# The first products of a conditioned trunk layer: conditioning one k-tile ahead, seven early load places in one ring, whole-float32 products for the first four k-tiles

## The chip, the cores and the metric

The kernel runs on one core of one Trainium2 chip. The metric is the device time of one execution in microseconds (us). TensorE (PE) does the matmuls, VectorE (DVE) and ScalarE (ACT) the elementwise work, GpSimd (POOL) a few small operations, and SyncE (SP) issues the loads from HBM. Each engine takes its instructions in the order in which they were recorded for it and waits where an operand isn't there yet.

## The reference, cut to what matters

One layer on x of 256 tokens by 2048 channels, float32, with one conditioning vector c:

```python
c_act = silu(c)
shift1, scale1, gate1, shift2, scale2, gate2 = split(c_act @ w_ada + b_ada, 6)   # w_ada 2048 x 12288
h = rms_norm(x, norm1_g) * (1 + scale1) + shift1
proj = h @ w_in + b_in                                # w_in 2048 x 8192
a_in, s_in, gates = split(proj, [2048, 4096])         # a: GLU, s: u and v, gates: 4096 wide
...                                                   # conv, LayerNorm, spatial mixing, merge
x = x + gate1 * (merged @ w_out)
...                                                   # up projection, conv, silu, down projection
```

The change lies in the first two lines (of which shift1 and scale1 are needed for h) and in the first part of h @ w_in.

## The kernel before, in words

All matrices are tiled by 128. The 2048 channels are 16 k-tiles; h is kept transposed, one tile of 128 channels by 256 tokens for each k.

A float32 product is made of three matmuls in a reduced type, float32r: an operand is split into a high part, rounded, and a low part, the rest (`split`, L135 to L137: ACT writes hi at L136, DVE lo at L137). `mm3` (L157 to L161) multiplies hi by hi, hi by lo and lo by hi into one PSUM tile. `load_raw` (L139 to L142) loads a block of weights, mostly 1 MB, into one of four places of 128 x 2048 with the tag `raw`; a pool gives each load the place that comes free first.

Ahead of the products, cact = silu(c) is spread over 128 partitions by PE and copied to `cbc` by DVE (L111). The mean squares of x are summed by ACT (L213, L214) and DVE (L215), POOL raises them to the power -1/2 (L117), and DVE scales two identity tiles with them, `diag` (L219). PE transposes and scales x by a matmul with diag (L206, tiles `trx`), and ACT copies the result to `xT` (L207), in four parts q = 0 to 3: two ahead of the loop, two inside its first round.

The loop over k ("first products", L304 to L333) then does, for each of the 16 k-tiles:

- two `ada_block`s (L181 load of 1 MB, L182 DVE product with cbc and sum), one for a column of 128 values of scale1 and one for shift1. Their loads go into three places of their own, the slots T5 to T7, in turn.
- gs (L309) and sh (L310) on DVE, h (L312) and its high part hH (L136) on ACT, its low part hL (L137) on DVE.
- the load of the block of weights a (2048 columns for k < 4, 1280 later), and its split into hi_a and lo_a.
- PE's products of that block and h into pa0 to pa3 and pv0, which collect all k; for k < 4 also into pd0 to pd2, which are copied to `gab` after k = 3 (L331).
- the job of that k from `jobs` (L294): for k = 4 to 8 a quarter of the gate's products (`gate_quarter`: load gq, split, 48 matmuls into two tiles pgq; the result goes to gab by an ACT copy at L271 or a DVE sum at L273), for later k such quarters and halves (`half_job`, tiles pg, copy L285).

Behind this loop come v, a, u, g (the other gate halves), so (the spatial branch's output, whole-float32 products straight from its loaded block, L589), co (the convolution branch's output), wo, and then up and down. In them, `pump` interleaves background work: convolution taps, and the other four adaLN blocks, whose loads use the four `raw` places too. A scheduler places the instructions of all this on the engines; their order on each engine is fixed when the program is built.

Of the kernel before, what the change touches and what calls it, by code (L numbers as in the profile page):

```python
# [10 lines left out]
F32 = mybir.dt.float32  # L11
F32R = mybir.dt.float32r
AF = mybir.ActivationFunctionType
ALU = mybir.AluOpType
# [3 lines left out]
P = 128  # L18
D = 2048
S = 256  # L20
NT = S // P
KT = D // P
# [14 lines left out]
NV = 2  # L37
# [3 lines left out]
RAW_BUFS = 4  # L41
# [6 lines left out]
C_BIN = C_BADA + 6 * KT  # L48
# [16 lines left out]
def trunk(ctx, tc, xin, cvec, rows, wada, wa0q, wa0, wa1, wv, wu, wg, wgq0, wgq1, wgq2, wso, wco, wsT, wout, wup0, wup, wdn, out):  # L65
    nc = tc.nc
    ctx.enter_context(nc.allow_low_precision(reason="exact two-part split of float32 operands"))
    keep = ctx.enter_context(tc.tile_pool(name="keep", bufs=1))
    wp = ctx.enter_context(tc.tile_pool(name="wp", bufs=1))
# [3 lines left out]
    def psum(name="ps"):  # L73
        return pp.tile([P, 512], F32, tag="ps", name=name)

    def slot(i, shape, name, dt=F32):

        return keep.tile(shape, dt, tag=f"T{i}", name=name)

    def t1(name, n=S):  # L80
        return tp.tile([P, n], F32, tag="t1", name=name, bufs=7)
# [4 lines left out]
    def small(n, name):  # L86
        return tp.tile([P, n], F32, tag=f"sm{n}", name=name, bufs=4)
# [4 lines left out]
    cv = keep.tile([P, NCOL], F32, tag="cv", name="cv")  # L92
    xs = [slot(t, [P, D], f"xs{t}") for t in range(NT)]
    for t in range(NT):
        nc.sync.dma_start(out=xs[t], in_=xin[:, t, :])
    nc.sync.dma_start(out=cv[:, KT:], in_=cvec[:, KT:])
    ident = keep.tile([P, P], F32, tag="ident", name="ident")
    make_identity(nc, ident)
    ones = keep.tile([P, P], F32, tag="ones", name="ones")
# [6 lines left out]
    def bcast_cols(dst, cols, n, name, copy=nc.scalar.copy):  # L106

        ps = psum(f"bc{name}")
        for i in range(n):
            nc.tensor.transpose(ps[:, i * P:(i + 1) * P], cols[:, i:i + 1].broadcast_to([P, P]), ident)  # L110
        copy(dst, ps[:, :n * P])  # L111

    def rsqrt(dst, v, name):

# [8 lines left out]
    def rms_rstd(ss, name):  # L123

        n = ss.shape[1]
        v = small(n, f"v{name}")
        nc.vector.tensor_reduce(v, ss, axis=AX.X, op=ALU.add)
        nc.vector.tensor_scalar(v, v, 1.0 / D, EPS, op0=ALU.mult, op1=ALU.add)
        r = small(n, f"r{name}")
        rsqrt(r, v, name)  # L130
        return r

    last = {}

    def split(hi, lo, src):  # L135
        nc.scalar.activation(hi, src, AF.Copy)  # L136
        return nc.vector.tensor_tensor(lo, src, hi.bitcast(F32), op=ALU.subtract)  # L137

    def load_raw(src, name):  # L139
        n = src.shape[-1]  # L140
        raw = wp.tile([P, 2048], F32, tag="raw", name=f"raw_{name}", bufs=RAW_BUFS)[:, :n]
        nc.sync.dma_start(out=raw, in_=src)  # L142
        return raw

# [12 lines left out]
    def mm3(ps, wH, wL, aH, aL, start, stop, **kw):  # L157

        nc.tensor.matmul(ps, wH, aH, start=start, stop=False, **kw)  # L159
        nc.tensor.matmul(ps, wH, aL, start=False, stop=False, **kw)  # L160
        nc.tensor.matmul(ps, wL, aH, start=False, stop=stop, **kw)  # L161
# [8 lines left out]
    cact = keep.tile([P, KT], F32, tag="cact", name="cact")  # L170
    nc.scalar.activation(cact, cc, AF.Sigmoid)
    nc.vector.tensor_tensor(cact, cact, cc, op=ALU.mult)
    cbc = keep.tile([P, D], F32, tag="cbc", name="cbc")
    for q in range(4):
        bcast_cols(cbc[:, q * 512:(q + 1) * 512], cact[:, 4 * q:4 * q + 4], 4, f"c{q}", nc.vector.tensor_copy)

    def ada_block(which, j, dst, w=None):

        if w is None:
            w = wp.tile([P, 2048], F32, tag="raw", name=f"ada{which}_{j}", bufs=RAW_BUFS)  # L180
        nc.sync.dma_start(out=w, in_=wada[which, j])  # L181
        nc.vector.scalar_tensor_tensor(w, w, 1.0, cbc, op0=ALU.mult, op1=ALU.mult, accum_out=dst)  # L182

    def ada_cols(which):
        return keep.tile([P, KT], F32, tag=f"mod{which}", name=f"mod{which}")

    def bada(which, a=0, b=KT):
        return cv[:, C_BADA + which * KT + a:C_BADA + which * KT + b]
# [20 lines left out]
    xT = [slot(2 + i, [P, 8, S], f"xT{i}") for i in range(2)]  # L209
    ss1 = tp.tile([P, NT, 2], F32, tag="ss1", name="ss1", bufs=1)  # L210
    nc.gpsimd.memset(ss1, 0.0)
    jk = [keep.tile([P, D], F32, tag=tag, name=f"jk{tag}") for tag in ("hH", "hL")]
    nc.scalar.activation(jk[0], xs[0], AF.Square, accum_out=ss1[:, 0, 0:1])  # L213
    nc.scalar.activation(jk[0][:, :D // 2], xs[1][:, :D // 2], AF.Square, accum_out=ss1[:, 1, 0:1])  # L214
    nc.vector.scalar_tensor_tensor(jk[1][:, D // 2:], xs[1][:, D // 2:], 1.0, xs[1][:, D // 2:], op0=ALU.mult, op1=ALU.mult, accum_out=ss1[:, 1, 1:2])  # L215
    r1 = rms_rstd(ss1, "1")
    diag = keep.tile([P, NT, P], F32, tag="rrow", name="diag")
    for t in range(NT):
        nc.vector.tensor_scalar_mul(diag[:, t, :], ident, r1[:, t:t + 1])  # L219
    for q in range(2):  # L220
        transposes(xs, xT, q, "x", diag)

# [7 lines left out]
    hH = keep.tile([P, KT, S], F32R, tag="hH", name="hH")  # L230
    hL = keep.tile([P, KT, S], F32R, tag="hL", name="hL")
# [4 lines left out]
    pa = [psum(f"pa{j}") for j in range(4)] + [psum(f"pv0{j}") for j in range(NV // 2)]  # L236
    sc1, sh1 = ada_cols(1), ada_cols(0)
# [4 lines left out]
    def gab_of(j):  # L242

        if j // 4 not in gab4:
            gab4[j // 4] = slot((0, 1, 4, 2)[j // 4], [P, 4, 2 * S], f"gab{j // 4}")
        return gab4[j // 4][:, j % 4, :]
# [36 lines left out]
    def half_job(j):  # L283
        def f():
            nc.scalar.copy(gab_of(j), gate_half(j, 0))  # L285
        return f
# [4 lines left out]
    def q1(i):  # L291
        return lambda: gate_quarter((2 * i, 2 * i + 1), 1, wgq1[i]) if i < 5 else gate_quarter((10,), 1, wgq2)

    jobs = {4: [q0(0)], 5: [q0(1)], 6: [q0(2)], 7: [q0(3)], 8: [q1(0), q1(5)], 9: [half_job(11)], 10: [q1(1), half_job(12)],  # L294
            11: [q1(2)], 12: [half_job(13)], 13: [q1(3), half_job(14)], 14: [q1(4)], 15: [half_job(15)]}
    pd = []

    def direct(ps, hi, lo, j, k, last_k):
        for half in range(2):
            cs = slice((2 * j + half) * P, (2 * j + half + 1) * P)  # L300
            mm3(ps[:, half * S:(half + 1) * S], hi[:, cs], lo[:, cs], hH[:, k, :], hL[:, k, :],
                k == 0 and half == 0, k == last_k, skip_group_check=True)

    for k in range(KT):  # L304
        c = slice(k, k + 1)
        for i, (which, dst) in enumerate(((1, sc1), (0, sh1))):
            ada_block(which, k, dst[:, c], slot(5 + (2 * k + i) % 3, [P, 2048], f"ada{which}_{k}"))
        gs, sh = small(1, f"gs{k}"), small(1, f"sh{k}")
        nc.vector.scalar_tensor_tensor(gs, sc1[:, c], bsc1[:, c], cv[:, C_G1 + k:C_G1 + k + 1], op0=ALU.add, op1=ALU.mult)  # L309
        nc.vector.tensor_tensor(sh, sh1[:, c], bada(0, k, k + 1), op=ALU.add)  # L310
        h = t1(f"h{k}")
        nc.scalar.activation(h, xT[k // 8][:, k % 8, :], AF.Identity, scale=gs, bias=sh)  # L312
        split(hH[:, k, :], hL[:, k, :], h)
        src = wa0q[k] if k < 4 else wa0[k - 4]
        n0 = src.shape[-1]
        raw = load_raw(src, f"a{k}")
        hi = wp.tile([P, 2048], F32R, tag="hi", name=f"hi_a{k}", bufs=HI_BUFS)[:, :n0]
        lo = wp.tile([P, 2048], F32R, tag="lo", name=f"lo_a{k}", bufs=HI_BUFS)[:, :n0]
        split(hi, lo, raw)
        for j in range(4 + NV // 2):  # L320
            direct(pa[j], hi, lo, j, k, KT - 1)
        if k == 0:
            for q in range(2, 4):
                transposes(xs, xT, q, "x", diag)
            pd += [psum(f"pd{j}") for j in range(QD)]
        if k < 4:
            for j in range(QD):
                direct(pd[j], hi, lo, 4 + NV // 2 + j, k, 3)
        if k == 3:
            for j in range(QD):  # L330
                nc.scalar.copy(gab_of(j), pd[j])  # L331
        for job in jobs.get(k, ()):
            job()  # L333
    gab = [gab_of(j) for j in range(KT)]


# [64 lines left out]
    def ln_steps():  # L401
# [24 lines left out]
        def s6():  # L426
            bcast_cols(crow, st["rr"], NT, "cr")
# [23 lines left out]
    for which, dst in ((2, g1c), (4, sc2), (3, sh2)):  # L451
        for j in range(KT):
            bg["ada"].append((2.25, lambda which=which, dst=dst, j=j: ada_block(which, j, dst[:, j:j + 1])))
# [32 lines left out]
    for j in range(8):  # L486
        if j < NV:
            ps = pa[4 + j // 2][:, (j % 2) * S:(j % 2 + 1) * S]
        else:
            ps = psum(f"pvc{j}")[:, :S]  # L490
# [54 lines left out]
    for j in range(4, 8):  # L545
        ps = psum(f"pa{j}")
# [18 lines left out]
    for j in range(8):  # L565
        ps = psum(f"pu{j}")
# [7 lines left out]
    for j in range(KT):  # L574
        ps = gate_half(j, 1)
        nc.vector.tensor_tensor(gab[j], gab[j], ps, op=ALU.add)
        pump("g", 5.15, 2.9)
        for half, jj in ((0, J_GA + j), (1, J_GB + j)):
            nc.scalar.activation(gab[j][:, half * S:(half + 1) * S], gab[j][:, half * S:(half + 1) * S], AF.Sigmoid,
                                 bias=cv[:, C_BIN + jj:C_BIN + jj + 1])  # L580


    for j2 in range(8):
        raw = load_raw(wso[j2], f"so{j2}")
        ps = psum(f"pso{j2}")
# [4 lines left out]
        for half in range(2):  # L590
            j = 2 * j2 + half
# [125 lines left out]
    for j in range(KT):  # L717
        bg["ada"].append((2.25, lambda j=j: ada_block(5, j, g2c[:, j:j + 1])))
# [172 lines left out]
```

## Time and profile before

| | |
|---|---|
| median of 3 runs | 1382.54 us (1378.96 to 1382.74) |
| the profiled execution, its own time | 1383.14 us |
| its span | 1381.4 us |
| PE busy | 1337.5 us, 97% |
| DVE, ACT busy | 1073.6 us, 653.4 us |
| mean TensorE clock granted | 0.986 of full speed |

The profile is one execution. In a timeline a row gives the start, the duration, the engine, the line, the operation, its output and inputs, the shape, how many instructions the row stands for, and in brackets how long the engine had been idle before it and what it waited for. In the table of waits the numbers are the microseconds in total, how often, and the longest. A matmul's duration includes its way through the array, so that the distance between two starts, and not the duration, says what one costs in a dense stream.

### The profile page before, as it was taken

What the parts mean: (1) busy time and instruction counts of PE and PEld (TensorE: products, weight loads), DVE (VectorE), ACT (ScalarE), POOL (GpSimd) and SP (SyncE); (2) the same over time, 40 slices, a digit from 0 to 9 for tenths busy, and PEclk for the clock granted to TensorE, in tenths of its full rate; (3) what the DMA queues carried; (4) which work ended last, traced back from release to release, by engine and by line L of the source; (5) the groups of instructions that cost most, each with busy time, mean ns of one, the idle gap of its engine ahead of it and who ended that gap; (6) DMA issues with size and microseconds to landing.
All of it is one profiled execution on the core that took longest, in us unless ns stands there. A gap on an engine that the chain in (4) does not pass through costs nothing.

```text
span 1381.4 us, 19730 instructions
## 1 busy us (share of the span) xinstructions
PE 1337.5 (97%) x8200; PEld 1197.3 (87%) x8200; DVE 1073.6 (78%) x1321; ACT 653.4 (47%) x770; POOL 6.4 (0%) x18
## 2 busy tenths in 40 slices
PE   5799999999999999998999999999999999999997
PEld 5799999999999898887888888888888888888885
DVE  5878899999999798888898887754456776776573
ACT  4344465545541344435555555543334555555451
POOL 0000000000000000000000000000000000000000
PEclk8899999999999999999999999999999999999999
DMA  8988876778786898885887775555555555555551
GB/s 347 361 350 340 362 294 254 263 269 287 294 306 259 307 353 334 318 337 207 298 300 275 276 272 183 185 181 190 199 190 183 186 192 196 188 183 187 192 200 61
DMA packets 49481, 350.89 MB, mean 254 GB/s; under 512 B 5616, under 2 KB 5616, under 8 KB 8176
## 3 DMA queue, kind: packets, MB, share of 16 engines
q1 hardware_dynamic: 49392, 349.63, 68.5%
q8 instruction: 64, 1.05, 0.3%
q14 instruction: 25, 0.20, 0.0%
HBM read 347.51 MB, written 2.10 MB: 253 GB/s over the span
## 4 chain that ended last, share of the span: by engine, by line
PE 90%; DVE 6%; ACT 2%; issue 1%; DMA 1%; POOL 0%; SPq 0%; ACTq 0%; POOLq 0%; DVEq 0%
PE pup L732 24%; PE pup L733 12%; PE pod L166 6%; PE pod L167 6%; PE pod L165 6%; PE pso L589 4%; PE pg L159 2%; PE pg L161 2%; PE pg L160 2%; DVE ada L182 2%; PE powo L167 2%; PE powo L166 2%; PE powo L165 2%; PE pa L160 2%; PE pa L161 2%; PE pa L159 2%
## 5 line engine op out<-in xcount | busy, mean ns | idle before, releaser
L137 DVE TENSOR_TENSOR lo_up<-raw_up,hi_up 128x2048 fp32r<-128x2048 f32 x88 | 201.5, 2290 | 84.6 <-ACT hi_up L136 84.6
L732 PE MATMUL pup<-h2hH,hi_up 128*128 128x512 f32 x704 | 252.6, 397 | 0.9 <-DVE h2hH L228 0.9
L732 PE MATMUL pup<-h2hL,hi_up 128*128 128x512 f32 x704 | 251.0, 395 | 0.0
L182 DVE SCALAR_TENSOR_TENSOR ada<-ada,cbc 128x2048 f32<-128x2048 f32 x96 | 218.3, 2285 | 7.3 <-DMA ada<-in 7.3
L136 ACT ACTIVATE hi_up<-raw_up 128x2048 fp32r<-128x2048 f32 x88 | 168.7, 1917 | 109.9 <-PE pup L732 84.1
L733 PE MATMUL pup<-h2hH,lo_up 128*128 128x256 f32 x704 | 198.6, 282 | 0.0
L733 PE MATMUL pup<-h2hL,lo_up 128*128 128x256 f32 x704 | 197.9, 281 | 0.0
L137 DVE TENSOR_TENSOR lo_d<-raw_d,hi_d 128x2048 fp32r<-128x2048 f32 x42 | 96.3, 2292 | 94.5 <-ACT hi_d L136 94.5
L732 PEld LDWEIGHTS pup<-h2hH,hi_up 128*128 128x128 f32 x704 | 133.2, 189 | 32.9 <-DVE h2hH L228 1.3
L732 PEld LDWEIGHTS pup<-h2hL,hi_up 128*128 128x128 f32 x704 | 132.3, 188 | 31.4
L733 PEld LDWEIGHTS pup<-h2hH,lo_up 128*128 128x128 f32 x704 | 132.9, 189 | 0.0
L136 ACT ACTIVATE hi_d<-raw_d 128x2048 fp32r<-128x2048 f32 x42 | 80.5, 1917 | 109.9 <-PE pod L167 90.4
L733 PEld LDWEIGHTS pup<-h2hL,lo_up 128*128 128x128 f32 x704 | 132.0, 188 | 0.0
L166 PE MATMUL pod<-lo_d,f 128*128 128x512 f32 x332 | 130.2, 392 | 0.0
L167 PE MATMUL pod<-hi_d,f 128*128 128x512 f32 x332 | 130.2, 392 | 0.0
L165 PE MATMUL pod<-hi_d,f 128*128 128x512 f32 x332 | 130.1, 392 | 0.0
L161 PE MATMUL pg<-hH,lo_g 128*128 128x256 f32 x336 | 93.8, 279 | 0.2 <-DVE lo_g L137 0.2
L159 PE MATMUL pg<-hH,hi_g 128*128 128x256 f32 x336 | 94.0, 280 | 0.0
L160 PE MATMUL pg<-hL,hi_g 128*128 128x256 f32 x336 | 93.7, 279 | 0.0
L376 DVE SCALAR_TENSOR_TENSOR yc<-apad,cv,yc 128x256 f32<-128x256 f32 x200 | 84.0, 479 | 0.8 <-ACT yc L374 0.6
L741 ACT ACTIVATE yv<-pl,cv 128x256 f32<-128x256 f32 x88 | 51.0, 597 | 64.1 <-DVE pl L740 64.1
L159 PE MATMUL pa<-hH,hi_a 128*128 128x256 f32 x256 | 69.3, 293 | 8.1 <-ACT hH L136 7.3
(224 smaller groups left out, 2808.1 us busy)
## 6 DMA issues: line engine op xcount, KB each, us to landing
ada<-in SPq DMA_DIRECT2D x96, 1024.0 KB, 5.1
raw_up<-in SPq DMA_DIRECT2D x88, 1024.0 KB, 4.8
raw_d<-in SPq DMA_DIRECT2D x44, 1024.0 KB, 4.8
raw_g<-in SPq DMA_DIRECT2D x21, 1024.0 KB, 5.1
raw_wo<-in SPq DMA_DIRECT2D x16, 1024.0 KB, 5.4
raw_a<-in SPq DMA_DIRECT2D x12, 1024.0 KB, 5.7
raw_gq<-in SPq DMA_DIRECT2D x9, 1024.0 KB, 8.2
raw_u<-in SPq DMA_DIRECT2D x8, 1024.0 KB, 4.8
```

The source lines that it names most:

```text
L136: nc.scalar.activation(hi, src, AF.Copy)
L137: return nc.vector.tensor_tensor(lo, src, hi.bitcast(F32), op=ALU.subtract)
L159: nc.tensor.matmul(ps, wH, aH, start=start, stop=False, **kw)
L160: nc.tensor.matmul(ps, wH, aL, start=False, stop=False, **kw)
L161: nc.tensor.matmul(ps, wL, aH, start=False, stop=stop, **kw)
L165: nc.tensor.matmul(ps, aH, wH, start=start, stop=False, **kw)
L166: nc.tensor.matmul(ps, aH, wL, start=False, stop=False, **kw)
L167: nc.tensor.matmul(ps, aL, wH, start=False, stop=stop, **kw)
L182: nc.vector.scalar_tensor_tensor(w, w, 1.0, cbc, op0=ALU.mult, op1=ALU.mult, accum_out=dst)
L376: nc.vector.scalar_tensor_tensor(ycf[:, j, :], src, cv[:, w0 + k:w0 + k + 1], ycf[:, j, :], op0=ALU.mult, op1=ALU.add)
L732: nc.tensor.matmul(ps, hi, hk.rearrange("p a s -> p (a s)"), start=(k == 0), stop=(k == KT - 1), skip_group_check=True)
L733: nc.tensor.matmul(ps[:, :S], lo, hk[:, 0, :], start=False, stop=(k == KT - 1), skip_group_check=True)
```

## The change

The conditioning of a k-tile (ada blocks, gs, sh, h, hH) becomes a function `condition`, and condition(k + 1) is recorded ahead of the products of k. The weights of k + 1 are loaded and split (`first_weights`) behind the job of k, and hL follows directly behind lo_a (`low_h`); for k < 4, hL stands behind the ada blocks of the next tile.

For k < 4 the weights are not split: one whole-float32 matmul with the loaded block and h takes the place of the three.

All loads of this stage go in turn into seven places, the four `raw` ones and T5 to T7. After the stage the four are used in turn, in the order in which the program asks for them, where a pool chose before.

The first load of cv, the table of small vectors, is cut to the columns that this stage needs; the rest is loaded at k = 3. The square sum of DVE is placed behind the copies to cbc, and the first ada blocks behind diag.

```diff
-    nc.sync.dma_start(out=cv[:, KT:], in_=cvec[:, KT:])
+    nc.sync.dma_start(out=cv[:, KT:C_BIN], in_=cvec[:, KT:C_BIN])
...
+    ring = {"n": 0, "all": RAW_BUFS + 3}
+    def raw_place(name):
+        i = ring["n"] % ring["all"]
+        ring["n"] += 1
+        return wp.tile([P, 2048], F32, tag=f"raw{i}", name=name, bufs=1) if i < RAW_BUFS else slot(5 + i - RAW_BUFS, [P, 2048], name)
...
-        raw = wp.tile([P, 2048], F32, tag="raw", name=f"raw_{name}", bufs=RAW_BUFS)[:, :n]
+        raw = raw_place(f"raw_{name}")[:, :n]
...
-    nc.vector.scalar_tensor_tensor(jk[1][:, D // 2:], xs[1][:, D // 2:], ...)
+    with tc.issue_after(last["cbc"].ins):
+        nc.vector.scalar_tensor_tensor(jk[1][:, D // 2:], xs[1][:, D // 2:], ...)
...
+    def condition(k):
+        c = slice(k, k + 1)
+        ada_block(1, k, sc1[:, c])
+        last["ada"] = ada_block(0, k, sh1[:, c])
+        ...                                   (gs, sh as before)
+        nc.scalar.activation(hs[k], xT[k // 8][:, k % 8, :], AF.Identity, scale=gs, bias=sh)
+        nc.scalar.activation(hH[:, k, :], hs[k], AF.Copy)
+
+    def first_weights(k):
+        if k < 4:
+            return load_raw(wa0q[k], f"a{k}"), None
+        ...                                   (load, hi and lo tiles as before)
+        with tc.issue_after(split(hi, lo, raw).ins):
+            low_h(k)
+        return hi, lo
+
+    def low_h(k):
+        nc.vector.tensor_tensor(hL[:, k, :], hs[k], hH[:, k, :].bitcast(F32), op=ALU.subtract)
...
+            if lo is None:
+                nc.tensor.matmul(dst, hi[:, cs], hs[k], start=first, stop=k == last_k, skip_group_check=True)
+            else:
+                mm3(dst, hi[:, cs], lo[:, cs], hH[:, k, :], hL[:, k, :], first, k == last_k, skip_group_check=True)
+
+    with tc.issue_after(last["diag"].ins):
+        condition(0)
+    parts = first_weights(0)
     for k in range(KT):
+        if k + 1 < KT:
+            condition(k + 1)
+        if k < 4:
+            with tc.issue_after(last["ada"].ins):
+                low_h(k)
...
+            nc.sync.dma_start(out=cv[:, C_BIN:], in_=cvec[:, C_BIN:])
         for job in jobs.get(k, ()):
             job()
+        if k + 1 < KT:
+            parts = first_weights(k + 1)
+    ring["all"] = RAW_BUFS
+    ring["n"] = 0
```

What this does to the order on the engines, at three places. In the rows below a name is a tile's, with the k or the block in it (h6 is h of k = 6; gq03 is the gate quarter of the tiles 3 and 4, the job of k = 4, and gq05 that of k = 5).

ACT, from h of k = 4 to the gate quarter of k = 5, before:

```order
L312 ACTIVATE h4_484<-xT0_114,sh4_481,gs4_480 128x256
L136 ACTIVATE hi_gq03_526<-raw_gq03_524 128x2048
L136 ACTIVATE hH_160<-h4_484 128x256
L136 ACTIVATE hi_a5_599<-raw_a5_597 128x1280
L312 ACTIVATE h5_593<-xT0_114,sh5_590,gs5_589 128x256
L136 ACTIVATE hH_160<-h5_593 128x256
L271 COPY gab0_470<-pgq03_530 128x512
L136 ACTIVATE hi_gq05_635<-raw_gq05_633 128x2048
```

and after:

```order
L316 ACTIVATE h4_319<-xT0_114,sh4_316,gs4_315 128x256
L136 ACTIVATE hi_a4_346<-raw_a4_344 128x1280
L317 ACTIVATE hH_160<-h4_319 128x256
L316 ACTIVATE h5_361<-xT0_114,sh5_358,gs5_357 128x256
L317 ACTIVATE hH_160<-h5_361 128x256
L136 ACTIVATE hi_gq03_396<-raw_gq03_394 128x2048
L136 ACTIVATE hi_a5_455<-raw_a5_453 128x1280
L279 COPY gab0_339<-pgq03_400 128x512
L279 COPY gab1_451<-pgq04_426 128x512
L316 ACTIVATE h6_470<-xT0_114,sh6_467,gs6_466 128x256
L317 ACTIVATE hH_160<-h6_470 128x256
L136 ACTIVATE hi_gq05_505<-raw_gq05_503 128x2048
```

The split of a gate quarter, which stood one row behind h of its own k, now stands behind h and hH of the next k; and that h stands behind both copies of the quarter before.

DVE, one round of the loop, from the low part of one gate quarter to that of the next, before:

```order
L137 TENSOR_TENSOR lo_gq05_636<-raw_gq05_633,hi_gq05_635 128x2048
L182 SCALAR_TENSOR_TENSOR ada1_6_691,mod1_167<-ada1_6_691,cbc_89 128x2048
L182 SCALAR_TENSOR_TENSOR ada0_6_694,mod0_168<-ada0_6_694,cbc_89 128x2048
L309 SCALAR_TENSOR_TENSOR gs6_697<-mod1_167,bsc1_169,cv_69 128x1
L310 TENSOR_TENSOR sh6_698<-mod0_168,cv_69 128x1
L137 TENSOR_TENSOR lo_a6_708<-raw_a6_705,hi_a6_707 128x1280
L137 TENSOR_TENSOR hL_161<-h6_701,hH_160 128x256
L137 TENSOR_TENSOR lo_gq07_744<-raw_gq07_741,hi_gq07_743 128x2048
```

and after:

```order
L137 TENSOR_TENSOR lo_gq03_397<-raw_gq03_394,hi_gq03_396 128x2048
L137 TENSOR_TENSOR lo_a5_456<-raw_a5_453,hi_a5_455 128x1280
L332 TENSOR_TENSOR hL_161<-h5_361,hH_160 128x256
L189 SCALAR_TENSOR_TENSOR ada1_6_460,mod1_167<-ada1_6_460,cbc_89 128x2048
L189 SCALAR_TENSOR_TENSOR ada0_6_463,mod0_168<-ada0_6_463,cbc_89 128x2048
L313 SCALAR_TENSOR_TENSOR gs6_466<-mod1_167,bsc1_169,cv_69 128x1
L314 TENSOR_TENSOR sh6_467<-mod0_168,cv_69 128x1
L137 TENSOR_TENSOR lo_gq05_506<-raw_gq05_503,hi_gq05_505 128x2048
```

The same seven operations; lo_a and hL have moved from behind gs and sh to the place ahead of the ada blocks, and the ada blocks belong to the tile after next.

SP, at the passage from so to co, before:

```order
L142 DMA raw_so7_4791<-in_13 128x2048
L181 DMA ada4_12_4813<-in_3 128x2048
L142 DMA raw_co0_4832<-in_14 128x2048
L181 DMA ada4_13_4897<-in_3 128x2048
L142 DMA raw_co1_4900<-in_14 128x2048
L142 DMA raw_co2_4965<-in_14 128x2048
```

and after:

```order
L150 DMA raw_so7_4648<-in_13 128x2048
L188 DMA ada4_12_4670<-in_3 128x2048
L188 DMA ada4_11_4645<-in_3 128x2048
L150 DMA raw_co2_4822<-in_14 128x2048
L150 DMA raw_co0_4689<-in_14 128x2048
L188 DMA ada4_13_4754<-in_3 128x2048
L150 DMA raw_co1_4757<-in_14 128x2048
```

The load of co2 now stands ahead of that of co0. By the places that the two programs give, co0 takes over the place of so5 before and that of so6 after, and co1 that of so6 before and that of so7 after.

More of the change, by code (lines that the diff above doesn't have):

```diff
@@ L110, in bcast_cols @@
             nc.tensor.transpose(ps[:, i * P:(i + 1) * P], cols[:, i:i + 1].broadcast_to([P, P]), ident)
-        copy(dst, ps[:, :n * P])
+        return copy(dst, ps[:, :n * P])
     def rsqrt(dst, v, name):
@@ L174, in trunk, with ada_block @@
     for q in range(4):
[L175 to L180, printed above, removed]
+        last["cbc"] = bcast_cols(cbc[:, q * 512:(q + 1) * 512], cact[:, 4 * q:4 * q + 4], 4, f"c{q}", nc.vector.tensor_copy)
+    def ada_block(which, j, dst):
+        w = raw_place(f"ada{which}_{j}")
         nc.sync.dma_start(out=w, in_=wada[which, j])
-        nc.vector.scalar_tensor_tensor(w, w, 1.0, cbc, op0=ALU.mult, op1=ALU.mult, accum_out=dst)
+        return nc.vector.scalar_tensor_tensor(w, w, 1.0, cbc, op0=ALU.mult, op1=ALU.mult, accum_out=dst)
     def ada_cols(which):
@@ L214, in trunk @@
     nc.scalar.activation(jk[0][:, :D // 2], xs[1][:, :D // 2], AF.Square, accum_out=ss1[:, 1, 0:1])
-    nc.vector.scalar_tensor_tensor(jk[1][:, D // 2:], xs[1][:, D // 2:], 1.0, xs[1][:, D // 2:], op0=ALU.mult, op1=ALU.mult, accum_out=ss1[:, 1, 1:2])
+    with tc.issue_after(last["cbc"].ins):
+        nc.vector.scalar_tensor_tensor(jk[1][:, D // 2:], xs[1][:, D // 2:], 1.0, xs[1][:, D // 2:], op0=ALU.mult, op1=ALU.mult, accum_out=ss1[:, 1, 1:2])
     r1 = rms_rstd(ss1, "1")
@@ L218, in trunk @@
     for t in range(NT):
-        nc.vector.tensor_scalar_mul(diag[:, t, :], ident, r1[:, t:t + 1])
+        last["diag"] = nc.vector.tensor_scalar_mul(diag[:, t, :], ident, r1[:, t:t + 1])
     for q in range(2):
@@ L296, in trunk @@
     pd = []
[L298 to L304, printed above, removed]
+    hs = {}
+    def condition(k):
         c = slice(k, k + 1)
-        for i, (which, dst) in enumerate(((1, sc1), (0, sh1))):
-            ada_block(which, k, dst[:, c], slot(5 + (2 * k + i) % 3, [P, 2048], f"ada{which}_{k}"))
+        ada_block(1, k, sc1[:, c])
+        last["ada"] = ada_block(0, k, sh1[:, c])
         gs, sh = small(1, f"gs{k}"), small(1, f"sh{k}")
@@ L310, in trunk, with direct @@
         nc.vector.tensor_tensor(sh, sh1[:, c], bada(0, k, k + 1), op=ALU.add)
[L311 to L316, printed above, removed]
+        hs[k] = t1(f"h{k}")
+        nc.scalar.activation(hs[k], xT[k // 8][:, k % 8, :], AF.Identity, scale=gs, bias=sh)
[3 more added lines that the diff above has]
+            return load_raw(wa0q[k], f"a{k}"), None
+        n0 = wa0.shape[-1]
+        raw = load_raw(wa0[k - 4], f"a{k}")
         hi = wp.tile([P, 2048], F32R, tag="hi", name=f"hi_a{k}", bufs=HI_BUFS)[:, :n0]
         lo = wp.tile([P, 2048], F32R, tag="lo", name=f"lo_a{k}", bufs=HI_BUFS)[:, :n0]
-        split(hi, lo, raw)
+        with tc.issue_after(split(hi, lo, raw).ins):
[3 more added lines that the diff above has]
+        nc.vector.tensor_tensor(hL[:, k, :], hs[k], hH[:, k, :].bitcast(F32), op=ALU.subtract)
+    def direct(ps, parts, j, k, last_k):
+        hi, lo = parts
+        for half in range(2):
+            cs = slice((2 * j + half) * P, (2 * j + half + 1) * P)
+            dst = ps[:, half * S:(half + 1) * S]
+            first = k == 0 and half == 0
+            if lo is None:
[5 more added lines that the diff above has]
+    parts = first_weights(0)
+    for k in range(KT):
+        if k + 1 < KT:
[3 more added lines that the diff above has]
+                low_h(k)
         for j in range(4 + NV // 2):
-            direct(pa[j], hi, lo, j, k, KT - 1)
+            direct(pa[j], parts, j, k, KT - 1)
         if k == 0:
@@ L327, in trunk @@
             for j in range(QD):
-                direct(pd[j], hi, lo, 4 + NV // 2 + j, k, 3)
+                direct(pd[j], parts, 4 + NV // 2 + j, k, 3)
         if k == 3:
```

## The prediction

> **What bounds the kernel now.** I read the page first, then PE's waits by time, then the busy time by stage.
>
> ```profile
> span 1381.4 us, 19730 instructions
> PE 1337.5 (97%) x8200; PEld 1197.3 (87%) x8200; DVE 1073.6 (78%) x1321; ACT 653.4 (47%) x770; POOL 6.4 (0%) x18
> PE 90%; DVE 6%; ACT 2%; issue 1%; DMA 1%; POOL 0%; SPq 0%; ACTq 0%; POOLq 0%; DVEq 0%
> ```
>
> PE is busy nearly throughout and carries 90% of the chain. Its waits from 200 us on, and then the larger ones before 200 us (us in total, times, longest):
>
> ```profile
> PE bcr L110 <- DVE r L121: 4.2, 1, 4.2
> PE pup L732 <- DVE h2hH L228: 0.9, 1, 0.9
> PE pvc L161 <- DVE lo_v L137: 0.6, 1, 0.6
> ```
>
> ```profile
> PE trx L206 <- DVE diag L219: 10.7, 1, 10.7
> PE pa L159 <- ACT hH L136: 7.3, 7, 1.7
> ...
> PE pgq L159 <- ACT hi_gq L136: 3.0, 1, 3.0
> ```
>
> After 200 us only 5.7 us of waits are left, so a microsecond won or lost in the first products reaches the end. Busy time by stretch:
>
> ```profile
> 33.70:57.90 24.20, 20.09 (x144) 18.87 (x144) 21.38 (x24) 8.06 (x9) 0.00 (x0) 0.93 0.89 361
> 57.90:65.90 8.00, 5.03 (x22) 4.77 (x22) 6.48 (x6) 4.50 (x6) 0.00 (x0) 0.67 1.01 397
> 65.90:107.90 42.00, 39.70 (x322) 38.65 (x320) 32.01 (x34) 20.06 (x24) 0.00 (x0) 0.98 0.88 345
> 107.90:198.40 90.50, 86.28 (x721) 84.43 (x719) 79.55 (x89) 42.25 (x48) 1.10 (x1) 1.00 0.83 330
> 300.00:400.00 100.00, 100.00 (x851) 100.00 (x851) 100.00 (x128) 51.90 (x59) 0.00 (x0) 1.00 0.80 290
> ```
>
> After the length come PE, PEld, DVE, ACT and POOL, then the granted clock. A split matmul costs 100.00 / 851 = 0.1175 us. The k-tiles 0 to 3 end at 57.9, the rounds with gate quarters (k = 4 to 8) run to about 107.9, and the rest of the stage ends at 198.4. I cost the change at these three marks.
>
> **The start, and k-tiles 0 to 3.** DVE, POOL and PE before the first product:
>
> ```profile
> 9.31 1.23 DVE L215 SCALAR_TENSOR_TENSOR jkhL<-xs 128x1024 f32<-128x1024 f32 x1 [6.19 <-DMA xs<-in]
> 10.46 0.08 DVE L215 DVE_READ_ACCUMULATOR jkhL<-xs 128x1 f32 x1
> 10.46 2.48 DVE L111 COPY cbc<-bcc 128x512 f32<-128x512 f32 x4
> ```
>
> ```profile
> 13.37 0.71 POOL L117 TENSOR_TENSOR r<-v,mhalf 128x2 f32<-128x2 f32 x1 [11.43 <-DVE v L128]
> ```
>
> ```profile
> 17.18 6.62 PE L206 MATMUL trx<-diag,xs 128*128 128x128 f32 x32 [10.66 <-DVE diag L219]
> 23.56 0.36 PE L159 MATMUL pa<-hH,hi_a 128*128 128x256 f32 x1
> ```
>
> The cbc copies move ahead of the square sum and the first ada reduction behind diag. One copy fits while xs lands; bsc follows it and waits for the cut cv load just behind xs (taken as 9.6). The other three copies (1.9) and the square sum (1.15) end at 12.7, so POOL starts at 13.2 instead of 13.37; after it no ada block (2.2) and no gs stand ahead of diag, and PE starts near 14.85 instead of 17.18. ACT now puts h0 behind all four xT copies: 14.85 + 6.62 + a copy + h0 is 22.6, or 21.8 if the clock rises earlier. I take 22.2 for the first product, instead of 23.56.
>
> Whole-float32 products are in the trace already, in the so stage (us, PE busy, count, clock):
>
> ```profile
> 420.00:483.00 63.00, 55.91 (x256) 1.00 0.76 288
> ```
>
> A 128x256 product is two of these records, 2 x 0.2184 = 0.437 us, against 3 x 0.1175 = 0.353 split. The Trainium skill ("FP8 and Floating Point Precision", TensorE Precision Notes) gives true float32 four passes; at 0.1175 that would be an estimated 0.47 and 2.1 us more over the stage. The trace's 0.437 decides.
>
> 64 products make 128 x 0.2184 = 28.0 us, and 32 records of transposes (0.1175) 3.75. With both weight splits of ACT and DVE gone and h one tile ahead, I see no wait between them. Their loads are 12 MB in 31.7 us, 397 GB/s, under the 426 GB/s that a row below shows at full load, and seven places have a lead when the products begin; the rest of cv, now loaded behind the ada blocks of k = 4, is read first behind the stage: the tiles end at T = 22.2 + 31.7 = 53.9 (53.4 to 54.4), **4.0 us earlier** than 57.9. The products themselves cost 5.4 us more; the waits they replace were larger.
>
> **From T to the first gate quarter.** ACT's copy and split, here beside the clock that follows PE's idle stretches:
>
> ```profile
> 57.94 0.59 ACT L331 COPY gab<-pd 128x512 f32<-128x512 f32 x1
> 58.42 0.60 ACT L312 ACTIVATE h<-xT,sh,gs 128x256 f32<-128x256 f32 x1
> ```
>
> ```profile
> 43.40:46.80 3.40, 3.40 (x18) 0.52 1.01 426
> 60.86:67.28 6.42, 6.41 (x28) 0.50 0.94 368
> ```
>
> Before, lo_gq of k = 4 starts at 60.9, 3 us behind T. After, ACT takes three pd copies, h4 and only then hi_a4; DVE's next rows are lo_a4, hL4, two ada blocks, gs5, sh5, and only then ACT does h5, hH5, hi_gq4. In rows: copy and h4 1.1, hi_a4 to lo_a4 1.3, lo_a4 1.4, hL4 0.3, ada 4.4, handoff 3.2 (rows below): lo_gq4 starts at T + 11.7 = 65.6, 4.7 us later than before. PE's idle stretches there (about 2.5 and 3.8 us) are as long as those that in the trace went ahead of the half clock (3.0 at 60.9). Half a clock for 3.4 us makes the quarter's products 1.7 us late, for 6.8 us 3.4, and ACT's two copies of them stand ahead of the next h: I add 1.7 (0 to 3.1).
>
> **The rounds of k = 4 to 8.** DVE's round now, and the handoff through ACT where an ada block directly precedes it:
>
> ```profile
> 95.70 2.29 DVE L137 TENSOR_TENSOR lo_gq<-raw_gq,hi_gq 128x2048 fp32r<-128x2048 f32 x1 [1.38 <-ACT hi_gq L136]
> 97.91 2.28 DVE L182 SCALAR_TENSOR_TENSOR ada<-ada,cbc 128x2048 f32<-128x2048 f32 x1
> ...
> 102.74 1.49 DVE L137 TENSOR_TENSOR lo_a<-raw_a,hi_a 128x1280 fp32r<-128x1280 f32 x1
> 104.47 0.42 DVE L137 TENSOR_TENSOR hL<-h,hH 128x256 fp32r<-128x256 f32 x1 [0.24 <-ACT hH L136]
> 106.28 3.43 DVE L137 TENSOR_TENSOR lo_gq<-raw_gq,hi_gq 128x2048 fp32r<-128x2048 f32 x2 [1.38 <-ACT hi_gq L136]
> ```
>
> ```profile
> 140.42 0.21 DVE L309 SCALAR_TENSOR_TENSOR gs<-mod,bsc,cv 128x1 f32<-128x1 f32 x1
> ...
> 143.64 2.29 DVE L137 TENSOR_TENSOR lo_gq<-raw_gq,hi_gq 128x2048 fp32r<-128x2048 f32 x1 [1.19 <-ACT hi_gq L136]
> ```
>
> Before, a round takes 106.28 - 95.70 = 10.58: while ACT makes h, hH and hi_gq, DVE has lo_a and hL to do. After, those two stand right behind lo_gq and the ada blocks come last, so DVE has nothing to do from gs to the next lo_gq, 143.64 - 140.42 = 3.2 us. The round is 2.2 + 1.4 + 0.3 + 4.4 + 3.2 = 11.6, **1.0 us longer, four times**. PE needs 78 x 0.1175 = 9.2 us a round, so it waits. lo_gq8 starts at 65.6 + 46.4 + 1.7 = 113.7, with PE as far as it was at 107.9: **+5.8 us**. The remaining stretch keeps its 90.5 us: DVE's rows leave waits of about 5 us, at the jobs of k = 10 and 13, for the 4.2 there now (-2 to +2). The 0.6 wait for lo_v has time to vanish.
>
> **The load places behind the stage.** The four places now go round in program order; before, each load took the one that came free first. At the so and co stages (SP, ACT, DVE, PE):
>
> ```profile
> 476.19 4.59 SPq L142 DMA_DIRECT2D raw_co<-in  x2
> ```
>
> ```profile
> 476.20 1.90 ACT L136 ACTIVATE hi_co<-raw_co 128x2048 fp32r<-128x2048 f32 x1
> ```
>
> ```profile
> 478.13 2.29 DVE L137 TENSOR_TENSOR lo_co<-raw_co,hi_co 128x2048 fp32r<-128x2048 f32 x1 [0.60 <-ACT hi_co L136]
> ```
>
> ```profile
> 482.61 0.47 PE L159 MATMUL pco<-aH,hi_co 128*128 128x256 f32 x1
> ```
>
> ```profile
> DMA to landing us min/median/max: 6.0/6.9/8.6
> ```
>
> co0 takes so5's place now, which PE leaves early, and co1 so6's: its issue at 476.19 shows when that came free. After, co0 gets so6's and stands behind co2 on SP; co2 takes bandwidth too. With 6.0 to landing it is there at 482.2; hi_co0 takes 1.8, lo_co0 2.3, so PE has it at 486.2 instead of needing it at 483.0: **+3.2** (0 if PE has something else to do, 6 with 8.6 to landing). DVE has put the so7 sums ahead of lo_co0, which end about then and add nothing. SP's other swapped loads wait less than their cover and cost nothing; were one of them late, it would cost the same few microseconds.
>
> **Sum.** 5.8 - 0.6 + 3.2 = +8.4. The profiled execution took 1383.14, 0.6 above the median 1382.54; on the median's level this is 1390.9, said as 1391.0.
>
> **Rivals.** Within 0.3% (4.1 us, about what a measurement of this kernel can tell) means 1378.4 to 1386.7.
>
> *B, the stretch behind k = 8 catches up.* Conditioning is a tile ahead and seven places load ahead, so the 4.2 us of waits in 107.9 to 198.4 go: 90.50 - 86.28 = 4.2, and the total is +4.2, 1386.7 or, with co0 on time, 1383.5. I put it at 1385. For it: PE's waits there, as those of all of k > 0, are mostly for hH (row above), just what is made earlier. Against: DVE has 79.6 us of work in these 90.5.
>
> *C, faster.* The rounds run at PE's 9.2 us, because the handoff hides behind work that I ordered wrongly: lo_gq8 is then at 65.6 + 36.8 = 102.4, 5.5 us early; with B's 4.2 and 0.6, less 3.2 at co0, that is 7 to 10 us, about 1375. DVE's own work is only 8.4 us a round. Against it: gs and sh stand behind both ada blocks, and lo_gq behind them. It decides as soon as DVE's idle time ahead of lo_gq falls below 0.8 us.
>
> *D, the clock.* The shorter bursts of PE let the clock fall in each round, not once: 3.4 us at half in four rounds is up to 1.7 x 4 = 6.8, less PE's 2.4 us of slack where the copies aren't waited for; I count 5, 1396. For: the half clock in 43.4 to 46.8 came behind a wait of 1.7. Against: 65.9 to 107.9 has waits up to 1.0 at clock 0.98. The Trainium skill ("TensorE: Matmul & The Clock Gate", Part 1) halves the rate after an idle window of some 3.4 us; by that rule two gaps of 1.2 a round would not do it, and the trace agrees so far.
>
> **Chances.** Forecast 0.56, D 0.11 (both slower), B 0.19, C 0.14. The range reaches over B to 1382 and, with co0 at its worst or D, to 1398; C lies outside.
>
> **What would show it.** Right: T near 54, then PE waiting some 4 us for hi_gq; DVE idle about 3 us ahead of each lo_gq of k = 5 to 8, rounds of 11.6; stage end near 204; a PE wait of some 3 us ahead of the first pco. Wrong: rounds at or under 10.6, no wait at co0, T later than 56 (the float32 products or ada loads too slow), or half the clock in every round.

## The result, and the profile after

The changed kernel took 1398.91 us (1397.73 to 1401.07, 4 runs) against 1380.75 us for the kernel before in the same rounds: ratio 1.0133, 95% interval 1.011 to 1.0157. Timed again later against other runs of the kernel before (1382.85 us), it took 1395.82 us (1392.81 to 1398.45, 6 runs): 1.0087, interval 1.0066 to 1.0108. The intervals just fail to overlap. The change costs between 0.7 and 1.6%, where 0.6% was forecast. The direction was right and the size too small, and the first result lies outside the range.

There are thus two profiles of the same changed kernel, called the first and the second below. Four marks place the loss; each is a start of a first product on PE, from the rows of the tiles pu, pso and pup.

| | first u product | from first so product to first up product | first up product | span |
|---|---|---|---|---|
| before | 284.7 | 210.1 | 630.5 | 1381.4 |
| changed, first profile | 294.5 (+9.8) | 217.6 (+7.5) | 647.8 (+17.3) | 1396.0 |
| changed, second profile | 291.0 (+6.3) | 217.7 (+7.6) | 644.5 (+14.0) | 1395.6 |

Between u and so nothing differs. Behind the first up product the first profile takes 748.2 us, the second 751.1 and the kernel before 750.9. Those 2.7 us are a difference between executions and not a gain of the change, so the first profile's span understates the loss.

The start did what was forecast. Two PE rows of the first profile, the transposes and the first whole-float32 products:

```profile
14.66 5.41 PE L213 MATMUL trx<-diag,xs 128*128 128x128 f32 x32 [7.89 <-DVE diag L227]
21.23 3.72 PE L341 MATMUL pa<-h,raw_a 128*128 128x256 f32 x16 [1.17 <-ACT h L316]
```

PE starts its transposes 2.5 us earlier than before, and its products at 21.2 instead of 23.6. The last pd copy, which marks the end of k-tile 3, and the rows behind it on ACT:

```profile
52.74 0.59 ACT L365 COPY gab<-pd 128x512 f32<-128x512 f32 x1 [0.28 <-PE pd L341]
53.22 0.60 ACT L316 ACTIVATE h<-xT,sh,gs 128x256 f32<-128x256 f32 x1
53.72 1.26 ACT L136 ACTIVATE hi_a<-raw_a 128x1280 fp32r<-128x1280 f32 x1
```

It starts at 52.7, in the second profile at 53.8; before, at 57.9. Up to here the change gains 4 to 5 us. Then DVE's low parts of the gate quarters of k = 4 to 8 in the first profile:

```profile
64.63 2.29 DVE L137 TENSOR_TENSOR lo_gq<-raw_gq,hi_gq 128x2048 fp32r<-128x2048 f32 x1 [2.92 <-ACT hi_gq L136]
...
76.81 2.29 DVE L137 TENSOR_TENSOR lo_gq<-raw_gq,hi_gq 128x2048 fp32r<-128x2048 f32 x1 [3.52 <-ACT hi_gq L136]
...
89.55 2.29 DVE L137 TENSOR_TENSOR lo_gq<-raw_gq,hi_gq 128x2048 fp32r<-128x2048 f32 x1 [4.08 <-ACT hi_gq L136]
...
101.13 2.29 DVE L137 TENSOR_TENSOR lo_gq<-raw_gq,hi_gq 128x2048 fp32r<-128x2048 f32 x1 [2.92 <-ACT hi_gq L136]
...
113.78 3.43 DVE L137 TENSOR_TENSOR lo_gq<-raw_gq,hi_gq 128x2048 fp32r<-128x2048 f32 x2 [4.00 <-ACT hi_gq L136]
```

The first three of these rows in the profile before (the last two, at 95.70 and 106.28, stand in the prediction):

```profile
60.85 2.29 DVE L137 TENSOR_TENSOR lo_gq<-raw_gq,hi_gq 128x2048 fp32r<-128x2048 f32 x1 [1.52 <-ACT hi_gq L136]
...
73.36 2.29 DVE L137 TENSOR_TENSOR lo_gq<-raw_gq,hi_gq 128x2048 fp32r<-128x2048 f32 x1 [3.49 <-ACT hi_gq L136]
...
85.14 2.29 DVE L137 TENSOR_TENSOR lo_gq<-raw_gq,hi_gq 128x2048 fp32r<-128x2048 f32 x1 [1.64 <-ACT hi_gq L136]
```

The rounds are now 12.2, 12.7, 11.6 and 12.7 us. Before, they are 12.5, 11.8, 10.6 and 10.6; there the clock was at half up to 67.4. DVE is now idle 2.9 to 4.1 us ahead of each row. The idle time of 2.9 is the forecast handoff; with it the round is 11.58, the forecast 11.6. The longer ones come through ACT:

```profile
70.84 0.59 ACT L279 COPY gab<-pgq 128x512 f32<-128x512 f32 x1 [5.09 <-PE pgq L169]
73.44 0.59 ACT L279 COPY gab<-pgq 128x512 f32<-128x512 f32 x1 [2.00 <-PE pgq L169]
73.92 0.60 ACT L316 ACTIVATE h<-xT,sh,gs 128x256 f32<-128x256 f32 x1
74.55 0.42 ACT L317 ACTIVATE hH<-h 128x256 fp32r<-128x256 f32 x1
74.88 1.90 ACT L136 ACTIVATE hi_gq<-raw_gq 128x2048 fp32r<-128x2048 f32 x1
```

sh of this round starts at 73.1 and takes 0.2 us, but h starts at 73.9, behind a copy that waited for PE. PE was late because its clock had fallen. Busy time and, behind the count, the granted clock in four stretches of the first and then of the second profile:

```profile
66.00:78.00 12.00, 11.10 (x79) 0.87 1.02 421
78.00:90.00 12.00, 11.21 (x77) 0.86 0.84 316
90.00:102.00 12.00, 10.31 (x81) 1.00 0.77 292
102.00:114.00 12.00, 10.90 (x75) 0.86 0.80 299
```

```profile
66.00:78.00 12.00, 12.00 (x78) 0.77 1.02 418
78.00:90.00 12.00, 10.03 (x79) 1.00 0.77 291
90.00:102.00 12.00, 10.29 (x80) 1.00 0.90 335
102.00:114.00 12.00, 10.09 (x82) 1.00 0.79 293
```

The program is the same: in one execution the clock falls in three of four rounds, in the other only in the first, after which its rounds are 11.57, 11.58 and 11.58 us long. What PE waits for is the same. So the rounds' loss has a fixed part, the order, and a part that differs from execution to execution, the clock.

Behind the stage, PE's waits from 210 us on:

```profile
PE bcr L110 <- DVE r L121: 5.2, 1, 5.2
PE pco L169 <- DVE lo_co L137: 1.8, 1, 1.8
PE pco L167 <- ACT hi_co L136: 1.7, 1, 1.7
PE pup L771 <- DVE h2hH L236: 0.9, 1, 0.9
```

The wait ahead of co is there, 3.5 us in all, where 3.2 was forecast; in the second profile it is 2.6 and 1.5, 4.1 us. The wait for r at the second norm has grown from 4.2 to 5.2: an ada block (637.53, 2.28 us) now stands between two rows of the residual on DVE. And co runs slowly behind its wait:

```profile
492.80:496.00 3.20, 0.50 (x2) 0.97 0.98 384
496.00:500.00 4.00, 3.17 (x15) 0.50 0.76 270
500.00:505.00 5.00, 5.00 (x34) 0.73 1.00 377
```

From the first so product to the first wo product it is 115.1 us (430.2 to 545.3) instead of 108.5 (420.4 to 528.9): 6.6 us more, of which 3.5 are the wait. The rest falls where the clock is at half, from 495.8 to 502.7.

### The profile page after: what moved, and what is told of

Same layout as the page of the kernel before. It is cut to its first block, busy times and chain, and to the rows that moved or that the text cites. A ratio compares the mean times of both kernels' runs of the same rounds, so it can differ in the third digit from the quotient of the medians.

```text
span 1396.0 us, 19599 instructions
## 1 busy us (share of the span) xinstructions
PE 1348.1 (97%) x8136; PEld 1206.0 (86%) x8136; DVE 1064.8 (76%) x1317; ACT 645.2 (46%) x766; POOL 6.4 (0%) x18
## 4 chain that ended last, share of the span: by engine, by line
PE 92%; DVE 3%; ACT 2%; DMA 1%; issue 1%; POOL 0%; SPq 0%; ACTq 0%; POOLq 0%; DVEq 0%
PE pup L771 24%; PE pup L772 12%; PE pod L175 6%; PE pod L174 6%; PE pod L173 6%; PE pso L628 3%; PE pg L167 3%; PE pg L169 3%; PE pg L168 3%; PE powo L173 2%; PE powo L174 2%; PE powo L175 2%; PE pa L167 2%; PE pgq L169 1%; PE pa L169 1%; PE pa L168 1%
## 5 line engine op out<-in xcount | busy, mean ns | idle before, releaser
L173 PEld LDWEIGHTS pod<-hi_d,f 128*128 128x128 f32 x332 | 62.3, 188 | 14.0
```

What stands on the lines that cost most here:

```text
L173: nc.tensor.matmul(ps, aH, wH, start=start, stop=False, **kw)
```

## The experiments

Theory: the loss is the order of the rounds from k = 4 on, and the turn of the load places behind the stage; each wait that they give PE is paid once as a wait and, where it brings the clock down, a second time. The rivals stand with each run. Times are medians, ratios are to the kernel before in the same rounds with 95% intervals.

| run | us | ratio | first u product | so to up |
|---|---|---|---|---|
| old order from k = 4 | 1382.26 | 0.9993 (0.9981 to 1.0006) | 278.6 | 217.4 |
| pool's choice of places | 1391.85 | 1.0066 (1.005 to 1.0082) | 292.3 | 210.2 |
| both | 1376.86 | 0.9953 (0.9938 to 0.9968) | 277.8 | 210.0 |
| filler ahead of co | 1395.95 | 1.009 (1.0073 to 1.0107) | 294.1 | 215.0 |
| filler ahead of quarters | 1395.77 | 1.0093 (1.0077 to 1.0109) | 292.5 | 216.1 |
| both fillers | 1396.33 | 1.0092 (1.0073 to 1.0111) | 292.6 | 215.4 |
| before, places in turn | 1391.41 | 1.0069 (1.0054 to 1.0085) | 285.4 | 218.5 |
| before, whole float32 | 1378.05 | 0.9966 (0.9953 to 0.998) | 282.4 | 210.1 |
| both, and k = 4 ahead | 1373.59 | 0.9932 (0.9918 to 0.9946) | 276.0 | 210.1 |

**The old order of the rounds (a change undone in part).**

```diff
-        if k + 1 < KT:
-            condition(k + 1)
+        if k >= 4:
+            condition(k)
+            parts = first_weights(k)
+        elif k + 1 < 4:
+            condition(k + 1)
...
-        if k + 1 < KT:
+        if k + 1 < 4:
             parts = first_weights(k + 1)
```

> The changed kernel with the k-tiles from 4 on in the order of before (condition, load and split, products and job of the same k); the start, the whole-float32 products, the seven places and the places behind the stage stay changed. Theory (the order of the rounds is what costs: the round of 11.6 us instead of 10.6, and PE idle in each round, which lets the clock fall to half for 3.4 us): the first u product, 9.8 us later than before in the changed kernel, comes 3 to 7 us earlier than before, since the four k-tiles still end 5 us earlier; with the 6.7 us at co and 1.0 at the second norm left, the time is 1 to 5 us over before, so 11 to 15 us under the changed kernel's +16. Rival (PE without its backlog of split products waits in any order): the first u product stays 4 us or more behind before, time over before by 12 or more.

The first u product comes at 278.6, 6.1 us earlier than before and 12 to 16 earlier than in the two profiles of the changed kernel. The order of the rounds is thus what the stage loses by. The time is that of before within 0.2%, a little better than the 1 to 5 us over it that were expected; what the places cost is still in it.

**The pool's choice of places.**

```diff
-        return wp.tile([P, 2048], F32, tag=f"raw{i}", name=name, bufs=1) if i < RAW_BUFS else slot(...)
+        return wp.tile([P, 2048], F32, tag="raw", name=name, bufs=RAW_BUFS) if i < RAW_BUFS else slot(...)
```

> The changed kernel with the four raw places given by the pool again, so that co0 is loaded ahead of co1 and co2. Theory (the fixed turn of places makes co0 late, the wait of 3.5 us for it drops the clock to half for 7 us, 3.2 more, and one more ada block ahead of the second norm costs 1.0): pco starts without a wait and at full clock, 6 to 8 us under the changed kernel. Rival 1 (the half clock in co has another cause): 3 to 4 us under it. Rival 2 (the wait is for bandwidth, not for the place): within 1 us of it.

The waits behind the first u product are those of before, the one at co gone:

```profile
PE bcr L110 <- DVE r L121: 4.2, 1, 4.2
PE pup L771 <- DVE h2hH L236: 0.9, 1, 0.9
```

From so to up it is 210.2 us, 7.4 less than in the changed kernel, as the theory said. In time the 6 to 8 us that were expected aren't shown by this run alone: the median is 4 us under the changed kernel's second timing and 7 under the first, and the interval of its ratio overlaps with that of the second. The clean comparison in time is that of the next run with the old order, in the same rounds and without overlap: 0.9953 against 0.9993, some 5 us.

**Both.** The two edits in one kernel.

> Both edits, old order from k = 4 on and the pool's choice of places. Theory: the two parts add up; what is left is the earlier end of the four k-tiles, so 3 to 7 us under before (0.995 to 0.998 of it). Rival (the gain of the first four k-tiles is taken back in later rounds, for the load or the ada blocks are late): within 2 us of before or over it.

The parts add up: 0.9953, some 6 us under before. The quarters' low parts of k = 4 to 8 in this kernel, and its clock:

```profile
57.44 2.29 DVE L137 TENSOR_TENSOR lo_gq<-raw_gq,hi_gq 128x2048 fp32r<-128x2048 f32 x1 [0.91 <-ACT hi_gq L136]
...
69.62 2.29 DVE L137 TENSOR_TENSOR lo_gq<-raw_gq,hi_gq 128x2048 fp32r<-128x2048 f32 x1 [1.38 <-ACT hi_gq L136]
...
101.14 3.43 DVE L137 TENSOR_TENSOR lo_gq<-raw_gq,hi_gq 128x2048 fp32r<-128x2048 f32 x2 [1.38 <-ACT hi_gq L136]
```

```profile
50.00:60.00 10.00, 7.21 (x36) 0.83 1.01 419
60.00:110.00 50.00, 46.03 (x383) 1.00 0.97 357
110.00:200.00 90.00, 85.98 (x722) 1.00 0.87 326
```

The first one starts 4.5 us behind the last pd copy, where it was 11.9 in the changed kernel, and three of the four rounds are between 10.4 and 10.6 us. The full clock from 60 us on is the other part: PE still waits 1 us a round, but with this order the clock holds.

**Useless work in PE's waits.** Ahead of co0, and ahead of the quarters:

```diff
         ps = psum(f"pco{j2}")
+        if j2 == 0:
+            for i in range(28):
+                nc.tensor.matmul(ps[:, :S], aH[:, i % 8, :P], aH[:, i % 8, :], start=True, stop=True)
```

> The changed kernel with 28 added matmuls of 0.1175 us (aH by aH into the bank of pco0, which the first true product overwrites) ahead of co0, in PE's wait for it: 3.3 us of work without use. Theory (the wait itself drops the clock): PE is busy in the wait, the clock stays at full, and co ends some 3 us earlier than in the changed kernel although PE has 3.3 us more to do; the wait for lo_co0 ends when it did. Rival (the half clock has another cause, or the added work delays the products): 0 to 3.5 us later than the changed kernel.

At co the theory holds. The clock in the same three stretches as above:

```profile
492.80:496.00 3.20, 3.16 (x27) 1.00 0.97 364
496.00:500.00 4.00, 3.60 (x30) 1.00 0.83 281
500.00:505.00 5.00, 5.00 (x44) 1.00 0.92 342
```

It stays at full, and from so to up it is 215.0 us instead of 217.6: PE does 3.3 us more and is through 2.6 earlier. The median, however, is that of the changed kernel's second timing, so the expected gain of some 3 us is not seen in the time; it is little beside the spread of single runs (1392.34 to 1397.86).

```diff
             hi, lo = parts[i]
+            if i == 0 and (kq, js[0]) not in ((1, 4), (1, 8), (1, 10)):
+                for n in range(12):
+                    nc.tensor.matmul(ps[:, :S], hH[:, 4 * kq + n % 4, :P], hH[:, 4 * kq + n % 4, :], start=True, stop=True)
```

> The changed kernel with 12 added matmuls of 0.1175 us (hH by hH into the bank of the quarter's first tile, overwritten by its first true product) ahead of the gate quarters of k = 4 to 8, 10 and 13, in PE's waits: 1.4 us of useless work each, about 10 us in all. Theory (the waits of each round drop the clock to half for 3.4 us, and the late copies on ACT then delay the next round): no half clock in 60 to 145 us, all rounds 11.6 us, the first u product 4 to 9 us earlier than in the changed kernel (there at 294.5). Rival (only the order of the rounds costs, the clock nothing): the first u product where it was or later by what of the 10 us doesn't fit into the waits.

This one decides nothing. Its rounds are 12.7, 11.58, 11.57 and 11.58 us, with the clock at 1.00 in 78 to 114, which looks like a proof. But the second profile of the unedited kernel has the same rounds, and its first u product is earlier still (291.0 against 292.5). Half the clock in the first round remained. The expected 4 to 9 us were missed.

> The changed kernel with both sets of added matmuls (12 ahead of the gate quarters that wait, 28 ahead of co0), 13 us of useless work. Theory (each wait is paid twice, once as a wait and once by the clock behind it): the two gains add up, 2 at the first u product and 2.6 in co, so 4 to 6 us under the changed kernel. Rival (one gain takes the other's place, or the work shows up elsewhere): within 2 us of the changed kernel.

That fell too: 1396.33 us, no gain. The fillers don't win back the clock's share in the rounds, and its size is known only as the difference between two executions (3.5 us at the first u product).

> The changed kernel without an edit, timed in more rounds, for the comparison with the edits. By the marks of its first profile it is 17.3 us behind before at the first up product, and the time differs by 15 to 19 us (1.011 to 1.014); the 14.6 us of that profile's whole span would be an execution whose up stage was 2.6 us shorter. Rival: the up stage is shorter in this kernel, and the difference stays near 14.6.

The ratio came out lower than expected, 1.0087, some 12 us, and the first up product comes 14.0 us later than before. The profile's up stage took what the kernel before takes (751.1 and 750.9 us), so the rival's reason is out.

**Before, with the four places in turn.**

```diff
+        i = ring["n"] % RAW_BUFS
+        ring["n"] += 1
-        raw = wp.tile([P, 2048], F32, tag="raw", name=f"raw_{name}", bufs=RAW_BUFS)[:, :n]
+        raw = wp.tile([P, 2048], F32, tag=f"raw{i}", name=f"raw_{name}", bufs=1)[:, :n]
```

> The kernel before with one edit: the four raw places go round in the order of the program, in its whole length. Theory: all of what the changed kernel loses behind the first products comes from this: pco waits some 3.5 us for hi_co0 and lo_co0, runs at half the clock for up to 7 us, and an ada block stands ahead of the second norm: 6 to 9 us over before. Rival (the loads are late only behind the changed first stage): within 2 us of before.

The fixed turn alone costs 0.69%. Its larger waits from 480 us on:

```profile
PE bcr L110 <- DVE r L121: 5.1, 1, 5.1
PE pco L166 <- ACT hi_co L136: 2.8, 1, 2.8
PE pco L168 <- DVE lo_co L137: 1.8, 1, 1.8
```

The cost doesn't need the changed first products: from so to up it is 218.5 us against 210.1.

**Before, with whole-float32 products for k < 4.**

```diff
+            if lo is None:
+                nc.tensor.matmul(ps[:, half * S:(half + 1) * S], hi[:, cs], h, start=k == 0 and half == 0, stop=k == last_k, skip_group_check=True)
+                continue
```

> The kernel before with one edit: whole-float32 products for k < 4 instead of split ones. Theory (the four k-tiles gain by what ACT and DVE no longer split, the conditioning ahead adds little): they end at 52 to 55 us instead of 57.9, and the time is 3 to 6 us under before. Rival (the earlier start and the conditioning ahead carry the gain of 5 us, and PE's 5.4 us more work takes the place of waits): they end at 57 us or later, the time within 2 us of before or over it.

The last pd copy starts at 54.6, and the time is 0.34% under before. From its first product (23.2) to that copy it takes 31.4 us, in the changed kernel 31.5: the conditioning ahead adds nothing within the four tiles. The change's gain there is the float32 products (3.3 us) and the earlier start (2 us in the first profile, 1 in the second).

**k = 4 ahead as well.** On top of both edits, k = 4 is conditioned and split during the products of k = 3, with the pd copies behind it on ACT:

```diff
+        if k == 3:
+            parts4 = first_weights(4)
+            last['hi4'] = last['hi']
...
-                nc.scalar.copy(gab_of(j), pd[j])
+                with tc.issue_after(last['hi4'].ins if j == 0 else last['pd'].ins):
+                    last['pd'] = nc.scalar.copy(gab_of(j), pd[j])
```

> As the run with both edits (old order from k = 4 on, the pool's choice of places), but k = 4 is conditioned, loaded and split while PE is at the products of k = 3, with its high part ahead of the pd copies on ACT. Theory (of the conditioning ahead only the passage from k = 3 to 4 is worth something, for PE waits 2.8 us for hH there): that wait falls under 0.5 us, DVE has lo_a4 done ahead of it, and the time is 2 to 4 us under the run with both edits. Rival (the rounds behind it are set by DVE, which gets no shorter): within 1 us of that run.

PE's waits in 50 to 110 us, of the run with both edits and then of this one:

```profile
PE pa L167 <- ACT hH L317: 6.7, 5, 2.8
```

```profile
PE pa L167 <- ACT hH L317: 4.0, 4, 1.0
PE pgq L169 <- DVE lo_gq L137: 0.8, 1, 0.8
```

The wait of 2.8 us is gone, the clock is at 1.00 from 50 to 110 us, and the first u product comes 1.8 us earlier than with both edits. At 1373.59 us and 0.9932 of before, this kernel has the lowest median of all; its interval overlaps with that of both edits, so the step between the two rests on the marks.

## Why the prediction was too small

| step | forecast | first profile | second profile |
|---|---|---|---|
| k-tiles 0 to 3 end earlier by | 4.0 | 5.2 | 4.1 |
| from there to lo_gq4 | 11.7 | 11.9 | 11.9 |
| lo_gq4 to lo_gq8 | 46.4 + 1.7 | 49.2 | 47.5 |
| first u product later by | 5.2 | 9.8 | 6.3 |
| so to up longer by | 3.2 | 7.5 | 7.6 |
| first up product later by | 8.4 | 17.3 | 14.0 |

The mechanisms were the forecast ones, and undoing the order of the rounds and the turn of the places showed both: the handoff of some 3 us, and the late load of co0. The part of the table up to lo_gq8 came out within 0.6 us (113.8 and 113.2 for 113.7). Its words "1.0 us longer, four times" don't hold beside the kernel before, whose first two rounds were themselves 12.5 and 11.8 us long: the four together grew from 45.4 to 49.2 and 47.5. The sum was spared this, because it took times from the start. (Two of its additions are 0.1 off: the round's five terms make 11.5, and 482.2 + 1.8 + 2.3 is 486.3.)

The step that failed is the term for co0, "486.2 instead of needing it at 483.0: +3.2": it prices the wait and not the clock behind it. The wait was 3.5 us, but behind it PE ran at half the clock for 6.8 us, and the filler experiment shows that this follows from the wait: with PE kept busy the clock stays full. The prediction counted half the clock once, 1.7 us at the first quarter, and nowhere else. From so to up, what is left beside the wait for co0 and the 1.0 us at the second norm is 3.0 us in the first profile, 2.5 in the second, and 2.0 in the run with the fillers ahead of the quarters, where co has the half clock for 3.41 us only. In the rounds and in the stretch behind k = 8 the half clock comes or stays away. In the first profile that stretch has the clock at 0.86 in three of its twelve-microsecond stretches, and it takes 4.5 us longer than forecast; in the second, one such stretch and 1.6 us. Of the rivals, the clock (0.11) was the one that came nearest. Its time, 1396, lies between the two results, though its account, a drop in every round, comes near only to the first profile, with three of four.

That the second part of that rival was set aside by the rule of an idle window was a mistake. The busy time of PE in the 3.4 us ahead of the half clock at 79.4 in the first profile, and in the half clock:

```profile
75.99:79.40 3.41, 2.20 (x15) 1.00 0.76 314
79.40:82.82 3.42, 3.42 (x18) 0.50 0.74 247
```

PE's three waits in the first row are 0.5, 0.4 and 0.3 us. That is far from an idle window as the Trainium skill has it ("TensorE: Matmul & The Clock Gate", Part 1), and still the clock fell. The profile before had such a case already, which the prediction names for the rival: the half clock from 43.5 on came after 3.41 us in which PE was busy for 1.55. The same page of the Trainium skill has the window run free of the program, and the traces agree. In every profile here the stretches at half clock between 25 and 660 us last 3.41 us or twice or three times that, and within one execution they all begin on one raster of that step; where the raster lies differs from execution to execution. In the second profile a step ends at 78.46 and so parts the first of the same three waits from the other two, and the clock stays:

```profile
75.05:78.46 3.41, 3.00 (x26) 1.00 1.01 417
78.46:81.88 3.42, 2.62 (x17) 1.00 0.47 167
81.88:85.29 3.41, 3.41 (x31) 1.00 0.86 310
```

Two more executions bear this out. The run with the filler at co alone has its first half clock behind k = 3 at 55.1, where the first profile has it at 55.5, and its rounds are those of the first profile (12.2, 12.7, 11.6 and 12.6 us). The run with the pool's places has it at 57.3, the second profile at 58.0, and its rounds are nearly those of the second (12.5, then three of 11.6). PE's busy time in a step is not the whole rule: after 2.20 us in 3.41 the clock fell, and after 2.13 from 88.70 on in the second profile it stayed.

A second, smaller step that failed is "SP's other swapped loads wait less than their cover and cost nothing". One ada block slipped behind the residual's first row on DVE and added 1.0 us at the second norm, in all the runs with the places in turn and in none with the pool.

Rival B's catching up did not come: the stretch behind k = 8 got longer, not shorter. Neither did C: gs and sh do stand behind both ada blocks, and DVE's idle time ahead of lo_gq was never under 2.9 us.

## What to carry to other kernels

Recording a stage one step ahead changes what stands behind what on the engines that take their work in order: here the split that PE waits for came to stand behind the next tile's whole conditioning, and the round grew by what DVE had done meanwhile. Where such a stage is not bound by PE, look in the order for the longest handoff that nothing covers, and make only those steps early that a wait in the trace asks for (here k = 4). Places given in a fixed turn tie a load to the one that had the place before, however late that one ends; and a wait of PE of a few microseconds should be priced with the half clock that may follow it. Where PE waits a little in every round, one profile shows one of several outcomes.

## What the runs showed of the hardware

The clock can fall after waits that leave PE busy for two thirds of the 3.41 us ahead of it (2.20 of 3.41), and in the run with both edits, with waits of 1 us a round, it held at 1.00 for 140 us (60 to 200). In each execution the falls lie on one raster of 3.41 us, whose place differs from one execution to the next; with it, the same waits bring the clock down or don't, and the two profiles of one kernel differ by 3.5 us at the first u product. How much work in a step is enough to keep the clock was not settled.
